# The output projection of a hybrid decoder layer, from eight dense tiles to seven block products

## The chip, the cores and the metric

The kernel runs on one core of a Trainium2 chip. A core has five engines that run their own instruction streams and meet only at semaphores: TensorE (PE, with its weight loads PEld), VectorE (DVE), ScalarE (ACT), GpSimd (POOL) and SyncE (SP, which only issues transfers here). The measure is the device time of one execution in microseconds (us), the median of several runs.

## The reference

One layer of a decoder, for 1024 positions of width 1024, all in float32:

```python
h = rmsnorm(x, mix_norm[l])
proj = h @ w_in[l]
q, k, v, su, sv, g_a, g_b = jnp.split(proj, splits, axis=-1)
y_att = sliding_window_attention(q, k, v, q_norm[l], k_norm[l], sinks[l])
y_sgu = chunked_spatial_gating(su, sv, sgu_norm[l], w_s[l], b_s[l])
merged = (jax.nn.sigmoid(g_a) * (y_att @ w_oa[l])
          + jax.nn.sigmoid(g_b) * (y_sgu @ w_ob[l]))
x = x + merged @ w_out[l]
x = x + conv_gated_mlp(rmsnorm(x, ffn_norm[l]), w_up[l], conv_w[l], conv_b[l], w_down[l])
```

The change is about `x + merged @ w_out` and about what it hands to the MLP: the rows of the new x times the gain `ffn_norm`, as right operands of the up projection. The RMS factor of that norm is one number per position, so it can be applied before or after the projection.

## The kernel before

Everything is kept transposed: channels on the 128 partitions, the 1024 positions along the free dimension, in two halves L and H of 512. Each float32 operand is used as a high and a low part: ACT rounds a copy (`copy_hi`), DVE or POOL subtracts it from the original, and each product is three matmuls, high x high, high x low, low x high (`mm3`, `prod`). A "split" below is this pair of a copy and a subtraction.

Most matrix products (gates, branches, up and down projection) are done in 2x2 blocks with seven products instead of eight: A11·B11, A12·B21, S1·T1, S2·T2, S3·T3, S4·B22, A22·T4, where the S are sums of weight blocks and the T sums of blocks of the right operand (`Blocks`, `Left`). For the two branch projections the S are formed in DRAM by accumulating transfers on POOL's queue (`wb_copy`, `wb_add`). The output projection alone is dense.

The stages around the change, in order:

- `gates()`: eight gate pairs, c = 0 to 7, whose tanh goes to DRAM.
- The branch projections: `B_UNITS`, eight units u of two jobs each (`branch`, `first` and `second`). A job splits a block of weights two jobs ahead, multiplies, and post-processes. The units u = 2, 4, 6, 7 belong to branch a; after each of them `m_add` adds the branches up to two row tiles of the merged matrix m and splits them into `mhi` and `mlo`, part of it late on POOL (`lo_late`). `un["hooks"]` puts further splits of the branches' right operands into the units.
- The output projection: eight jobs (`out_tile`, the last one `last_tile`), one per row tile d of 128 output channels in the order `D_ORDER`. Each is a dense product over all eight k, 48 matmuls. The first two tiles leave out k = 6 and 7, whose m comes last, and make them up later (`rest`). `post` adds the result to x, multiplies with gain and RMS factor of the first norm (`rstd_b`) into h, stores x, and forms the right operands of the MLP's up projection in `comb`: splits of B11, T1, B21, B22, T3 at once, T2 and T4 as raw sums that `first_pair` splits.
- `mlp()`: `first_pair` is the first pair of column tiles of the up projection, seven products of 12 matmuls, with the square sums of x in it (`ssq_cols`); 21 pairs follow, then the down projection.

`run_jobs` goes through the jobs: it issues the matmuls of job i, the load of job i + 4, the split for job i + 2, and what is left of job i, its post-processing. The program order of each engine is the order in which these functions are called (`tc.manual_schedule`): an instruction that waits holds back all that stand behind it on its engine. The split weights have two buffers ("wh" and "wl"), so the split for job i + 2 waits until TensorE has finished job i. SBUF has seven large slots that take turns under the tag "Y", PSUM four tiles of two banks each, from which `PS` takes the next in turn.

## Time and profile before

| | |
|---|---|
| median of 3 runs | 1174.04 us (1173.48 to 1174.11) |
| the profiled execution | 1174.47 us |
| its span | 1172.8 us |
| granted TensorE clock | 1.0 of full speed |
| bytes moved by DMA | 192.84 MB, mean 164 GB/s |
| largest idle time of TensorE from 330 to 600 us | 0.3 us, behind a POOL subtraction of weights |

How to read it: the busy time of an engine counts its instructions, not its waits. A matmul's duration in the records is longer than the distance to the next, since matmuls are pipelined; the time of a stretch of matmuls is read from first to first. In rows of a timeline the columns are start, duration, engine, line, operation, output and inputs, shape, count, and in brackets the idle time before it with what ended it. In rows of groups they are line, engine, operation, output and inputs, shapes, count, then busy time, mean duration in ns, and idle time before with what ended it. In rows of windows they are stretch, length, busy time and count of PE, PEld, DVE, ACT and POOL, the granted clock, the share of the DMA engines and GB/s. In rows of DMA issues the last columns are the size and the time from issue to landing.

### The profile page before, as it was taken

The page shows a single profiled execution, that of the slowest core. Times are in us where ns is not written, and L with a number is a line of the kernel's source. Part 1 is how long each engine was busy: PE and PEld are TensorE (multiplying, and loading weights), DVE is VectorE, ACT ScalarE, POOL GpSimd, SP SyncE. Part 2 cuts the span into 40 slices and gives each one's busy share as a digit, 9 for nine tenths or more (in the row PEclk, how much of TensorE's full clock was granted, in tenths as well). Part 3 has the DMA queues.
Part 4 walks back from the last instruction along what each step waited for, and adds up shares of the span by engine and source line. Part 5 has one row for each costly group of instructions (what it writes and reads, how often), then busy time and mean ns, then how long its engine had stood idle before and what let it go on. Part 6 is the DMA issues. An engine that isn't in the chain of part 4 may idle for free.

```text
span 1172.8 us, 15805 instructions
## 1 busy us (share of the span) xinstructions
PE 1164.2 (99%) x5832; PEld 987.3 (84%) x5832; DVE 848.3 (72%) x982; ACT 562.4 (48%) x868; POOL 631.1 (54%) x434
## 2 busy tenths in 40 slices
PE   9999999999999999999999999999999999999998
PEld 9899999888888878888888888888888888888887
DVE  6777746734446876778779778887888797875674
ACT  6665568643437543435544443444444455425231
POOL 1667574598883863454876767676767640000000
PEclk9999999999999999999999999999999999999999
DMA  9310155265737762554564545554555268966471
GB/s 365 108 37 21 64 184 190 84 203 174 203 103 254 238 203 96 180 153 126 144 167 131 146 133 162 137 163 111 171 135 162 81 209 304 363 218 198 161 234 64
DMA packets 82237, 192.84 MB, mean 164 GB/s; under 512 B 9328, under 2 KB 17008, under 8 KB 82032
## 3 DMA queue, kind: packets, MB, share of 16 engines
q1 hardware_dynamic: 74304, 171.78, 42.6%
q0 software_dynamic: 7456, 15.73, 8.4%
q10 hardware_dynamic: 400, 4.33, 1.1%
q8 instruction: 46, 0.75, 0.3%
q14 instruction: 31, 0.25, 0.1%
HBM read 151.17 MB, written 49.02 MB: 171 GB/s over the span
## 4 chain that ended last, share of the span: by engine, by line
PE 87%; DVE 4%; POOL 3%; ACT 2%; issue 2%; DMA 2%; SPq 0%; DVEq 0%; POOLq 0%; ACTq 0%
PE pz L1085 49%; PE pd L1880 10%; PE pdy L1880 8%; PE px L94 2%; PE px L92 2%; PE px L93 2%; PE pu L94 1%; PE pu L92 1%; PE pu L93 1%; PE pv L542 1%; PE pq L92 1%; PE pq L94 1%; PE pq L93 1%; PE sc L467 1%; PE sc L470 1%
## 5 line engine op out<-in xcount | busy, mean ns | idle before, releaser
L1085 PE MATMUL pz<-T,qh 128*128 128x512 f32 x472 | 145.6, 390 | 0.0
L1085 PE MATMUL pz<-B,ph 128*128 128x512 f32 x352 | 109.6, 392 | 0.1
L1085 PEld LDWEIGHTS pz<-T,qh 128*128 128x128 f32 x472 | 88.5, 188 | 18.6 <-ACT u L910 0.3
L1044 POOL TENSOR_TENSOR pl<-lp,ph 128x1024 fp32r<-128x1024 f32 x30 | 74.2, 2472 | 52.9 <-ACT ph L88 52.9
L1085 PE MATMUL pz<-T,ql 128*128 128x512 f32 x236 | 91.8, 389 | 0.0
L1044 POOL TENSOR_TENSOR ql<-lq,qh 128x1024 fp32r<-128x1024 f32 x30 | 76.7, 2557 | 9.1 <-ACT qh L88 9.1
L1085 PEld LDWEIGHTS pz<-B,ph 128*128 128x128 f32 x352 | 65.1, 188 | 15.8 <-ACT x L1720 2.8
L1103 DVE TENSOR_TENSOR pz<-pz,rstd_b 128x1024 f32<-128x1024 f32 x60 | 73.9, 1232 | 4.5 <-ACT rstd_b L142 2.5
L1085 PE MATMUL pz<-T,s3h 128*128 128x512 f32 x232 | 71.4, 389 | 0.0
L1085 PE MATMUL pz<-y,wjh 128*128 128x512 f32 x224 | 69.5, 391 | 0.6 <-POOL y L1258 0.3
L1085 PE MATMUL pz<-B,pl 128*128 128x512 f32 x176 | 68.5, 389 | 0.0
L1880 PE MATMUL pd<-bh,ah 128*128 128x512 f32 x176 | 68.5, 389 | 0.0
L1880 PE MATMUL pd<-bl,ah 128*128 128x512 f32 x176 | 68.5, 389 | 0.0
L1880 PE MATMUL pd<-bh,al 128*128 128x512 f32 x176 | 68.5, 389 | 0.0
L1085 PE MATMUL pz<-B,AX 128*128 128x512 f32 x264 | 63.4, 389 | 0.0
L1085 PE MATMUL pz<-T,AX 128*128 128x512 f32 x264 | 63.4, 389 | 0.0
L1044 POOL TENSOR_TENSOR s3l<-lq,s3h 128x512 fp32r<-128x512 f32 x20 | 26.0, 1298 | 61.3 <-ACT s3h L88 61.3
L1085 PEld LDWEIGHTS pz<-T,AX 128*128 128x128 f32 x264 | 49.6, 188 | 10.3
L1085 PEld LDWEIGHTS pz<-B,AX 128*128 128x128 f32 x264 | 49.6, 188 | 10.3
L88 ACT ACTIVATE AX<-lr 128x1024 fp32r<-128x1024 f32 x22 | 23.4, 1063 | 70.0 <-POOL lr L646 70.0
L1575 DVE SCALAR_TENSOR_TENSOR tg<-pz,cp,tg 128x1023 f32<-128x1023 f32 (+1 forms) x44 | 56.2, 1278 | 0.8
L1575 DVE SCALAR_TENSOR_TENSOR tv<-pz,cp,tv 128x1023 f32<-128x1023 f32 (+1 forms) x44 | 56.2, 1278 | 0.8
(352 smaller groups left out, 3524.2 us busy)
## 6 DMA issues: line engine op xcount, KB each, us to landing
lp<-wup SPq DMA_DIRECT2D x22, 512.0 KB, 3.7
lq<-wup SPq DMA_DIRECT2D x22, 512.0 KB, 4.1
ra<-wdown SPq DMA_DIRECT2D x44, 256.0 KB, 4.5
b<-T SPq DMA_DIRECT2D x44, 256.0 KB, 3.9
lq<-wup POOLq DMA_DIRECT2D x42, 256.0 KB, 5.3
B<-tv SPq DMA_DIRECT2D x33, 256.0 KB, 2.3
T<-tt SPq DMA_DIRECT2D x33, 256.0 KB, 2.1
b<-B SPq DMA_DIRECT2D x33, 256.0 KB, 3.7
```

Source lines behind the costliest of these rows:

```text
L88: return nc.scalar.activation(dst, src, AF.Copy, scale=scale)
L92: nc.tensor.matmul(out, wh, mh, start=first, stop=False, **kw)
L93: nc.tensor.matmul(out, wh, ml, start=False, stop=False, **kw)
L94: nc.tensor.matmul(out, wl, mh, start=False, stop=last, **kw)
L467: nc.tensor.matmul(o[g], qs[:, g, c], kTh[:, g, ks], start=t2 == 0, stop=False, skip_group_check=True)
L470: nc.tensor.matmul(o[g], qs[:, g, c], kTl[:, g, ks], start=False, stop=True, skip_group_check=True)
L542: nc.tensor.matmul(o, vhl[:, kb, g, :], w[:, 2 * g:2 * g + 2, :], start=i == 0 and g == 0, stop=i == len(ops) - 1, skip_group_check=True)
L1044: nc.gpsimd.tensor_tensor(l, r, h.bitcast(F), op=ALU.subtract)
L1085: nc.tensor.matmul(o, p[:, k, :], m, start=not more and k == 0 and j == 0, stop=k == nk - 1 and j == 2, skip_group_check=True)
L1103: nc.vector.tensor_tensor(z, z, rstd_b, op=ALU.mult)
L1575: nc.vector.scalar_tensor_tensor(t[:, j:], p[:, 0:1024 - j], cw[:, ci, 2 - j:3 - j], t[:, j:], op0=ALU.mult, op1=ALU.add)
L1880: nc.tensor.matmul(o[d], p[:, k - k0, m], q[:, k - k0, :], start=new and k == 0 and j == 0, stop=k == HK - 1 and j == 2, skip_group_check= ...
```

## The change

The output projection becomes seven block products as well, with its own order. Its matmuls run product by product: a step s takes one product over the four output tiles d of half the channels, as two jobs of two tiles each, 24 matmuls a job, so 14 jobs (numbers 16 to 29 of the list, called j = 0 to 13). The results gather in two sets of four PSUM quarters, X and Y:

- step 0: X = A11·B11, and ACT copies X to Y
- step 1: Y += A12·B21, which is quarter 11 of the result
- step 2: X += S2·T2; ACT copies X to Y; DVE keeps X with x21
- step 3: Y += S1·T1; DVE keeps Y with x22
- step 4: Y += S4·B22, which is quarter 12
- step 5: X = S3·T3, with what was kept quarter 22
- step 6: X += A22·T4, with what was kept quarter 21

The lower half comes out with the opposite sign, so that all four weight sums are additions; `final` turns it.

```diff
+    def wo_copy(j):
+        i, x = divmod(j, 2)
+        if x == 0:
+            d_wo.append(dr.tile([512, 1024], F, tag=f"wo{i}", name=f"wo{i}"))
+        nc.scalar.dma_start(d_wo[i][256 * x:256 * x + 256], a["wo"][i + x].rearrange("e p m -> (e p) m"))
+
+    def wo_add(j):
+        e, o = d_wo
+        x, y = slice(0, 256), slice(256, 512)
+        out, src = ((o[y], a["wo"][3].rearrange("e p m -> (e p) m")), (e[y], o[y]), (e[x], e[y]),
+                    (o[x], a["wo"][2].rearrange("e p m -> (e p) m")))[j]
+        nc.gpsimd.dma_start(out, src, accum_op=ALU.add, max_dma_last_dim=4096)
```

`wo_copy` is called in the gate pairs 1 to 4, `wo_add` at the start of the units 0 to 3. `m_add` no longer splits whole rows; it keeps m raw (`mraw`) and makes the block operands, some in it, some in hooks of the units 6 and 7, some in the first output jobs:

```diff
+        un["hooks"][6, "x"] = lambda: m_split("T1", 0)
+        un["hooks"][6, 0] = lambda: m_split("T1", 1)
+        un["hooks"][7, 0] = lambda: (m_split("B22", 0), m_split("B21", 0))
...
         for e, z in enumerate((q.zg, q.zv)):
             c = 2 * j + e
+            nc.vector.tensor_tensor(mraw[i][:, c % 4, :], ms.pop(c), z, op=ALU.add)
+        if i == 0:
+            m_split("B11", g)
+        else:
+            if u == 7:
+                for e in (0, 1):
+                    m_split("B21", g, ks=slice(2 * g + e, 2 * g + e + 1))
+        m_sum(("T1", "T2")[i], g)
```

The output jobs themselves, with the work that is put beside their matmuls:

```diff
+    O_STEPS = (("A11", "B11", "X"), ("A12", "B21", "Y"), ("S2", "T2", "X"), ("S1", "T1", "Y"), ("S4", "B22", "Y"),
+               ("S3", "T3", "X"), ("A22", "T4", "X"))
+    O_WORK = {
+        0: lambda: (m_split("T2", 0), out_load("11"), out_load("21")),
+        1: lambda: (m_split("T2", 1), m_split("B22", 1), out_load("22")),
+        2: lambda: (m_sum("T3", 0), m_sum("T3", 1), m_sum("T4", 0), m_sum("T4", 1), out_load("12")),
+        3: lambda: m_split("T4", 0, nc.gpsimd),
+        4: lambda: (m_split("T4", 1, nc.gpsimd), w0.load_p(), w0.load_s3(), w0.load_q()),
+        5: lambda: (b11(0), b11(1), m_split("T3", 0)),
+        6: lambda: (b11(2), b11(3), w0.adds()),
+        7: lambda: m_split("T3", 1),
+        8: lambda: w0.sums_r(),
+        9: lambda: w0.split_s3(),
+    }
+    def final(n, d, p, out, sign):
+        nc.vector.scalar_tensor_tensor(out, p, 0.5 * sign, ob[n][:, d, :], op0=ALU.mult, op1=ALU.add)
+    def o_post(s, d):
...
+        if s == 4:
+            g, ng = gain("12", d)
+            final("12", d, Yb, Yb, 1.0)
+            keep("12", d, Yb)
+            nc.scalar.activation(A, Yb, AF.Copy, scale=g)
+            stt(B, Yb, ng, B, ALU.add)
+            square("12", d, Yb, Yb)
+            right_split("T1", d, B, nc.vector)
+        if s == 5:
+            g, ng = gain("22", d)
+            final("22", d, X, Yb, -1.0)
+            right_split("B22", d, Yb, nc.vector, g)
+            keep("22", d, Yb)
+            stt(A, Yb, ng, A, ALU.add)
+            stt(B, Yb, ng, B, ALU.subtract)
+            square("22", d, Yb, Yb)
+        if s == 6:
+            g, ng = gain("21", d)
+            final("21", d, X, X, -1.0)
+            right_split("B21", d, X, nc.vector, g)
+            keep("21", d, X)
+            stt(X, X, g, B, ALU.add)
+            square("21", d, ob["21"][:, d, :], pools["fp"].tile([128, 512], F, tag="sqt", name=nm("sqt")))
...
+            O_WORK.get(j, lambda: None)()
+            yield
+            if s == 0:
+                if j == 0:
+                    ob["Y"] = [p[:, c] for p in (PS("pY"), PS("pY")) for c in (L, H)]
+                for d in (2 * e, 2 * e + 1):
+                    nc.scalar.copy(ob["Y"][d], ob["X"][d])
             else:
+                if s == 6:
+                    (w0.split_p, w0.split_q)[e]()
+                for d in (2 * e, 2 * e + 1):
+                    o_post(s, d)
+            if j == 11:
+                for d in range(4):
+                    right_split("T3", d, ob["A"][:, d, :], nc.vector)
+            if j == 12:
+                for d in range(4):
+                    right_split("T2", d, ob["B"][:, d, :], nc.vector)
```

Here `keep` is a copy on ACT and a store, `square` a square on ACT and, but for the first tile, a sum on DVE, `stt` one DVE operation, `right_split` a copy on ACT and a subtraction on the engine named. x is taken without the factor `rstd_b`, so `ssq_cols` no longer divides by it. `first_pair` has the order A11, S3, S1, A12, S4, S2, A22 and splits T4 straight from X; the MLP's first left operand is loaded and split within the output jobs instead of in a job of its own. The rotating tag "Y" becomes seven fixed slots Y0 to Y6, and the down projection takes its first four PSUM quarters from the other pool. In `run_jobs` every split now stands between a job's matmuls and its post-processing:

```diff
-        for i in range(len(jobs) - 1):
+        for i in range(len(jobs)):
             m = jobs[i][2](job_w.pop(i))
             next(m)
-            if i == 17:
-                job_split(18)
-                next(m)
-            if i:
+            if 0 < i < 16:
                 job_load(i + 4)
-            if i != 16:
-                job_split(i + 2)
-            if lo_late:
-                lo_late.pop(0)()
+            job_split(i + 2)
+            if i >= 16:
+                job_load(i + 4)
             for _ in m:
                 pass
```

349 lines of the change are left out of this document (166 added, 183 removed).

## The prediction

> **What bounds the kernel now.** I read the page first (busy time, chain of waits), then TensorE's timeline, the windows of the stages, the groups with shapes kept apart, and last the timelines of DVE, ACT and POOL where the change cuts in.
>
> ```profile
> span 1172.8 us, 15805 instructions
> ...
> PE 1164.2 (99%) x5832; PEld 987.3 (84%) x5832; DVE 848.3 (72%) x982; ACT 562.4 (48%) x868; POOL 631.1 (54%) x434
> ...
> PE 87%; DVE 4%; POOL 3%; ACT 2%; issue 2%; DMA 2%; SPq 0%; DVEq 0%; POOLq 0%; ACTq 0%
> ```
>
> TensorE is busy 99% of the span and carries 87% of the chain: a matmul taken away is time gained, and any wait put before a matmul is time lost, since no later slack gives it back.
>
> ```profile
> 447.48 0.39 PE L92 MATMUL px<-mh,wjh 128*128 128x512 f32 x1
> ...
> 535.09 0.61 PE L1085 MATMUL pz<-B,ph 128*128 128x512 f32 x2
> ...
> 555.99 0.61 PE L1085 MATMUL pz<-B,ph 128*128 128x512 f32 x2
> ```
> ```profile
> L94 PE MATMUL px<-mh,wjl 128*128 128x512 f32 x128 | 49.9, 390 | 0.3 <-POOL wjl L109 0.3
> L109 POOL TENSOR_TENSOR wjl<-wj,wjh 128x1024 fp32r<-128x1024 f32 x7 | 17.5, 2499 | 31.1 <-ACT wjh L88 31.1
> L88 ACT ACTIVATE B<-h 128x512 fp32r<-128x512 f32 x12 | 7.3, 629 | 26.5 <-DVE h L1483 20.8 <-DVE h L1523 5.7
> L1439 DVE TENSOR_TENSOR B<-h,B 128x512 fp32r<-128x512 f32 x9 | 6.0, 690 | 1.4 <-ACT B L88 1.4
> ```
>
> The output projection runs from 447.48 to 535.09: 87.6 us for 3x128 = 384 matmuls, 0.2275 us each (a record of 0.39 is a pipelined duration, not an interval), with 0.3 us idle. The first pair of the MLP takes 20.9 more, to 555.99. TensorE waits for nothing there because each dense tile lasts 48 matmuls, 10.9 us: its weight split and its post-processing fit beside it.
>
> **The change, part by part.** Times t count from the start of the output stage.
>
> *Removed:* 384 matmuls become 7 products x 4 tiles x 4 k x 3 = 336. The stage would last 336 x 0.2275 = 76.4: **-11.2 us**. Two small DVE operations in the row-norm go too; at nothing, TensorE doesn't wait for them. The job, the unit in which weights are split two ahead, halves to 24 matmuls, 5.46 us.
>
> *Prices:*
> ```profile
> 456.04 2.36 DVE L1393 TENSOR_TENSOR ml<-m,mh 128x1024 fp32r<-128x1024 f32 x2
> 478.54 1.15 ACT L88 ACTIVATE B<-h 128x512 fp32r<-128x512 f32 x2 [1.53 <-DVE h L1483]
> 479.60 0.62 ACT L88 ACTIVATE T<-h 128x512 fp32r<-128x512 f32 x1
> 424.67 2.57 POOL L1320 TENSOR_TENSOR wjl<-wj,wjh 128x512 fp32r<-128x512 f32 x2 [3.36 <-ACT wjh L88]
> 535.23 0.63 ACT L88 ACTIVATE B<-h 128x512 fp32r<-128x512 f32 x1 [2.67 <-DVE h L1523]
> 535.90 0.69 DVE L1439 TENSOR_TENSOR B<-h,B 128x512 fp32r<-128x512 f32 x1 [0.70 <-ACT B L88]
> ```
> DVE: 0.69 for 512 columns, 0.61 behind another, 1.17 for 1024. ACT: 0.53 behind another (479.60 - 478.54 for two), 0.63 alone, so about 1.0 for 1024. POOL: 1.29 a half, 2.4 for 1024. The last two rows are a **round trip**: DVE stands idle 0.70 while ACT makes the high part that DVE subtracts. The blocks are scheduled by hand, so every engine keeps the program's order.
>
> *(1) Weight sums in DRAM.* Four copies of 1 MB on ACT's queue in the gates: nothing, TensorE is full there and the eight earlier copies cost ACT only their issue. Four accumulating DMAs on POOL's queue in units 0 to 3:
> ```profile
> 385.55 4.05 POOL L1320 TENSOR_TENSOR wjl<-wj,wjh 128x512 fp32r<-128x512 f32 x2 [0.43 <-DMA wj<-wb]
> ...
> 393.90 2.40 POOL L1258 TENSOR_TENSOR y<-ta,y 128x1024 fp32r<-128x1024 f32 x1
> ```
> ```profile
> 396.35 0.50 PE L1085 MATMUL pz<-y,wjh 128*128 128x512 f32 x1 [0.26 <-POOL y L1258]
> ```
> ```profile
> wb<-wb POOLq DMA_DIRECT2D x1, 1024.0 KB, 14.4
> ```
> ```profile
> wb<-wb POOLq DMA_DIRECT2D x1, 1024.0 KB, 10.7
> ```
> ```profile
> L944 POOL DMA_DIRECT2D wb<-wb x6: 787/838/1093, 246.3 to 338.7; - x6
> ```
> TensorE already waits 0.26 for POOL's subtraction of 393.90, so there POOL's delay is TensorE's. The second add comes ahead of 385.55, the third ahead of 393.90, and the third reads what the second writes. Issued at 385.1, the second lands 10.7 to 14.4 later, 397.6 in the middle; then 0.84 to issue, 2.4 to subtract: 400.9 instead of 396.3. **+4.6 us** (2.8 to 6.5). Without that wait only two issues count, 1.3, the lower end. Behind the waiting instruction stand that subtraction and the weight splits of units 2 and 3. [...]
>
> *(2) The boundary.*
> ```profile
> 443.67 0.69 DVE L646 TENSOR_TENSOR x<-x,pz 128x512 f32<-128x512 f32 x1 [1.04 <-PE pz L1085]
> ...
> 447.98 0.68 DVE L1354 TENSOR_TENSOR pz<-x,pz 128x512 f32<-128x512 f32 x1
> ...
> 453.70 2.35 DVE L1387 TENSOR_TENSOR m<-m,pz 128x1024 f32<-128x1024 f32 x2
> ```
> ```profile
> 519.51 1.60 POOL L646 TENSOR_TENSOR lr<-lq,lp 128x512 f32<-128x512 f32 x1 [2.63 <-issue]
> 519.87 1.79 DVE L1439 TENSOR_TENSOR T<-h,T 128x512 fp32r<-128x512 f32 x1
> 521.19 1.61 POOL L646 TENSOR_TENSOR lr<-lp,lr 128x512 f32<-128x512 f32 x1
> 521.58 1.77 DVE L650 SCALAR_TENSOR_TENSOR T2f<-h,h 128x512 f32<-128x512 f32 x1
> ```
> DVE is nearly full in units 6 and 7. Added ahead of the addition of 447.98: T1's sum and splits in units 5 and 6 (they push the start at 443.67 back by 2.3, of which 1.04 was idle), and in unit 7 T2's sum and the splits of B22 and B21, 3.5, in place of a subtraction of 1.4. So 447.98 becomes 452.4, and the last sums of the branches end at 460.4 (t 12.9) instead of 456.05. ACT stands before them with B21's copies; behind these in its queue are T2's copy (1.0), the weight split of job 2 (1.0) and the copies X to Y, which job 2 accumulates onto: Y at t 16.1, POOL's first half of the low weights at 16.7. Job 2's third matmul was due at 11.4: **+5.4**. With nothing pushed back in units 5 and 6, it would be 3.0.
>
> After t 12.9 DVE has eight operations of 1.17 and two of 0.65 ahead of job 2's first `final`: B21, T2, B22, then `O_WORK[2]`'s four sums. That is t 23.6. But the last four rows show POOL and a DVE operation with both inputs in SBUF exclude each other and take turns (1.29 becomes 1.6, 0.69 becomes 1.8). Five POOL halves and their gaps fall between: t 31.2. Then ACT's six copies (to 35.2), T4's copy (36.1), POOL's T4 subtraction, which stands ahead of the weights (38.6), and a weight half, 39.9: job 5's third matmul, due at 33.2. **+6.8**, and 1.2 more for T4's other half before job 6. Without turns this part costs nothing; I take the rows. Part (2): **+13.4** (3 to 14).
>
> *(3) Post-processing and first pair.* Count from the end of job 8, step 4's first half (t' = 0). Per tile d, in order on DVE:
> - step 4: `final`, `stt`, wait for ACT's three operations, square sum, T1's low part: 3.7. Four tiles and a weight split between: to 15.3.
> - step 5: `final` 0.7, round trip 0.7, low part, two `stt` (0.61 each), round trip for the square 0.7, sum 0.65: 4.6. To 33.7; T3's four low parts to 36.2.
> - step 6: `final`, round trip, low part, `stt`, sum: 3.3.
>
> A job gives two tiles 5.46; these need 7.4, 9.2 and 6.6. TensorE waits because step 6 accumulates onto X, which step 5's `final` must have read: the last tile's at t' 29.8, so the stage ends at 32.6 instead of 27.3. Next late is the MLP's first left operand: `split_p` stands on ACT behind T3's copies (36.35), POOL adds 2.4: t' 38.85, product to 41.1. S3·T3 to 43.85. `split_q` stands on ACT behind step 6's first half (to 42.8) and T2's copies, so to 45.3; POOL waits for T2's last low part and adds 2.4: 47.8, S1·T1 to 50.1, A12·B21 to 52.8. `split_r` stands behind step 6's second half (ACT's last square at 51.1), x1's copy and two of T4's (52.7), takes 1.0 on ACT and 2.4 on POOL: S4·B22's third matmul at 56.15. Then 10 matmuls, S2·T2, the 1.8 of the square sums and A22·T4: 65.6, against 27.3 + 20.9 = 48.2. **+17.4 us.** Ends: with DVE's 63 operations (15 in step 4, 20 in step 5, 16 in step 6, 12 low parts) at 0.65 and no round trip it has 41 us of work where 43.7 are left before A22·T4: 0 to 3. Above: `split_r` also waits for a row's store out of its slot, +2. I take 17.4, since the round trip is a row.
>
> *(4) At nothing:*
> ```profile
> 447.50:535.00 87.50, 87.23 (x385) 71.94 (x384) 62.82 (x57) 28.32 (x37) 36.94 (x21) 1.00 0.45 142
> ```
> 3 MB more weight loads, under a DMA share of 0.45 in this stage (next to last column); fixed slots; the psum rotation of the last stage. If that cover fails, a late weight load costs what it is late.
>
> Sum: -11.2 + 4.6 + 13.4 + 17.4 = **+24.2**. The profiled execution took 1174.47 (span 1172.8 and 1.67 around); that is 0.43 above the median of 1174.04, so 1198.2.
>
> **Rivals.**
> 1. *The posts keep pace* (faster). If a tile's post goes at DVE's issue interval, 0.61, because ACT's copies are ready when DVE comes to them, steps 4 to 6 need at most 5 x 0.61 = 3.1 a tile, and DVE's backlog stays off the weights: -11.2 + 1.3 + up to 4, 1164 to 1168. It decides at 2.73 us per tile. For it: DVE is only 72% busy overall, and the posts of before cause no wait of TensorE. Against: the 0.70 idle in the row of 535.90.
> 2. *Half the loss.* The queues catch up in the MLP's first pair or the turns are not taken: 0 to 5 of part (2), 8 to 12 of part (3): 1175 to 1186.
> 3. *It cancels.* One part alone bites, about 11 us: 1172 to 1176.
> 4. *DMA congestion adds.*
> ```profile
> 381.00:390.00 9.00, 9.00 (x41) 7.46 (x40) 8.08 (x9) 6.02 (x9) 8.57 (x6) 1.00 0.73 234
> ```
> ```profile
> q0 software_dynamic: 7456, 15.73, 8.4%
> ```
> The DMA's share is 0.7 there already. The page gives the software queue 15.73 MB and 8.4% of the span, 6.3 us of all engines per MB; four adds are 25 us of all engines where 0.3 of the some 40 us of units 0 to 3 is free, 12. Late weights could add 6: up to 1208. It is the top of my range.
>
> That the products aren't saved is no rival: the loops count 336.
>
> **How the numbers follow.** Forecast, with congestion inside, 1186 to 1208: 0.62. Half the loss: 0.14. Cancels: 0.08, nearly all of it within 0.2%. Posts keep pace: 0.16. A measurement tells 0.2%, 2.3 us, from no change. Faster 0.16, same 0.07, slower 0.77. Range 1172 to 1208, which leaves out the faster case and a little above.
>
> **What would show it.** Right: TensorE idle about 4 us before S2·T2 of unit 2, released by POOL; 5 before the second step, released by ACT or POOL; a gap in job 5 behind T4; gaps of 2 in step 6 released by DVE; and 3 to 7 before A11, S1 and S4 of the first pair, released by POOL. Wrong: 336 matmuls in under 80 us, or a first pair of 21. What would break it most is an order on DVE or ACT other than the program's.

## The result, and the profile after

The change makes the kernel slower: 1227.16 us, median of 6 runs (1223.01 to 1230.37), beside 1174.07 (1173.48 to 1176.15) for the kernel before. The ratio is 1.045, with a 95% interval from 1.0429 to 1.0472. Forecast were 1198.2 with a range up to 1208: the sign was right, the size, +53.1 instead of +24.2, was not, and the time lies outside the range.

The profiled execution of the kernel after took 1226.57. Its page, with the span, TensorE's busy time, the granted clock in 40 slices and the chain by engine:

```profile
span 1224.7 us, 15874 instructions
...
PE 1171.8 (96%) x5784; PEld 988.5 (81%) x5784; DVE 861.1 (70%) x1019; ACT 594.8 (49%) x938; POOL 642.5 (52%) x448
...
PEclk9999999999999999987999999999999999999999
...
PE 75%; DVE 9%; ACT 5%; POOL 5%; issue 3%; DMA 2%; DVEq 0%; ACTq 0%; POOLq 0%
```

The 48 matmuls are gone (5832 became 5784), so the expected 11.2 us were saved. But TensorE's share of the chain fell from 87% to 75%, and DVE's rose from 4% to 9%. The second surprise is in the clock line: two slices, between 520 and 582 us, stand below 9.

TensorE's timeline of after, all waits over 1.4 us between 370 and 600 us (start, duration, ..., and in brackets the wait before the row and what ended it):

```profile
401.57 0.50 PE L1099 MATMUL pz<-y,wjh 128*128 128x512 f32 x1 [2.60 <-POOL y L1275]
...
419.22 0.73 PE L1099 MATMUL pz<-y,wjh 128*128 128x512 f32 x2 [2.58 <-ACT x L1356]
...
442.69 0.73 PE L1099 MATMUL pz<-y,wjh 128*128 128x512 f32 x2 [2.51 <-ACT x L1356]
...
475.19 1.22 PE L1611 MATMUL pY<-mB,wjh 128*128 128x512 f32 x2 [3.25 <-ACT pY L1620]
...
494.79 0.73 PE L1611 MATMUL pX<-mT,wjh 128*128 128x512 f32 x2 [1.56 <-ACT wjh L88]
...
497.93 0.50 PE L1611 MATMUL pX<-mT,wjl 128*128 128x512 f32 x1 [2.41 <-POOL wjl L1542]
...
546.36 1.19 PE L1611 MATMUL pX<-mT,wjh 128*128 128x512 f32 x2 [7.75 <-DVE pY L1509]
...
557.51 1.19 PE L1611 MATMUL pX<-mT,wjh 128*128 128x512 f32 x2 [3.78 <-DVE pY L1509]
...
583.49 1.22 PE L1099 MATMUL pz<-T,s3h 128*128 128x512 f32 x2 [13.64 <-ACT x L1735]
```

These nine sum to 40.1. With six more (1.35 us at 277.87 in the gates, and five of 0.4 to 0.9) the waits of TensorE from 250 to 640 us come to 44.9; in the kernel before they were 0.7.

The rows that follow the last of these waits, from the same timeline:

```profile
584.51 0.63 PE L1099 MATMUL pz<-T,s3l 128*128 128x512 f32 x1
584.93 1.05 PE L1099 MATMUL pz<-T,s3h 128*128 128x512 f32 x2
...
587.49 0.63 PE L1099 MATMUL pz<-T,s3h 128*128 128x512 f32 x2
587.96 0.39 PE L1099 MATMUL pz<-T,s3l 128*128 128x512 f32 x1
```

From 584.51 to 584.93 one matmul takes 0.42 us; from 587.49 to 587.96 two take 0.47. So behind the wait TensorE first runs at half speed. Read row by row, seven such stretches follow the waits, lasting 3.4 to 6.1 us and losing 1.5 to 2.9 us each against 0.2275 us a matmul, together 12.9 us. Behind the waits of 2.58, 2.51 and 2.41 the stretch begins only 0.8 to 1.5 us after the wait. The windows of the output stage with the first pair, before and then after, show the same in the clock (next to the DMA share):

```profile
460.00:565.00 105.00, 104.73 (x478) 86.96 (x477) 76.43 (x72) 41.53 (x56) 52.76 (x31) 1.00 0.47 141
```
```profile
460.70:565.90 105.20, 85.92 (x337) 68.00 (x337) 72.14 (x83) 57.18 (x97) 50.92 (x34) 0.90 0.43 143
565.90:605.50 39.60, 23.76 (x101) 18.42 (x101) 17.16 (x27) 16.54 (x27) 12.29 (x8) 0.83 0.33 93
```

The account of the span's +51.9 is then: -11.2 matmuls, +44.2 waits (44.9 - 0.7), +12.9 half speed, and 6.0 not followed further. No engine became a bound: DVE is busy 72 of 105 us in the stage that stalls. It waits as well.

### The profile page after: what moved, and what is told of

It reads as the page before. It is cut to its first block, busy times and chain, and to the rows that moved or that the text cites. A ratio compares the mean times of both kernels' runs of the same rounds, so it can differ in the third digit from the quotient of the medians.

```text
span 1224.7 us, 15874 instructions
## 1 busy us (share of the span) xinstructions
PE 1171.8 (96%) x5784; PEld 988.5 (81%) x5784; DVE 861.1 (70%) x1019; ACT 594.8 (49%) x938; POOL 642.5 (52%) x448
## 4 chain that ended last, share of the span: by engine, by line
PE 75%; DVE 9%; ACT 5%; POOL 5%; issue 3%; DMA 2%; DVEq 0%; ACTq 0%; POOLq 0%
PE pz L1099 44%; PE pdx L1962 10%; PE pd L1962 7%; DMA lq<-wga 1%; PE pu L94 1%; PE pu L92 1%; PE pu L93 1%; PE pv L542 1%; POOL pl L1058 1%; PE pq L92 1%; PE pq L94 1%; PE pq L93 1%; PE pY L1611 1%; POOL lr L646 1%; DVE mraw L1438 1%
## 5 line engine op out<-in xcount | busy, mean ns | idle before, releaser
L1962 PE MATMUL pdx<-bh,ah 128*128 128x512 f32 x176 | 68.6, 390 | 0.1
L1962 PE MATMUL pdx<-bh,al 128*128 128x512 f32 x176 | 68.5, 389 | 0.0
L1962 PE MATMUL pdx<-bl,ah 128*128 128x512 f32 x176 | 68.5, 389 | 0.0
L1099 PEld LDWEIGHTS pz<-T,s3h 128*128 128x128 f32 x232 | 44.4, 192 | 23.4 <-ACT x L1735 14.1
L1340 POOL TENSOR_TENSOR wjl<-wj,wjh 128x512 fp32r<-128x512 f32 (+1 forms) x32 | 39.1, 1243 | 41.7 <-ACT wjh L88 41.7
L646 DVE TENSOR_TENSOR pz<-pz,u 128x512 f32<-128x512 f32 x37 | 25.9, 700 | 45.7 <-ACT u L1111 39.4
L1058 POOL TENSOR_TENSOR AX<-lr,AX 128x1024 fp32r<-128x1024 f32 x22 | 53.5, 2432 | 8.6 <-ACT AX L88 8.6
```

Of the source, the lines that this page charges most:

```text
L646: eng.tensor_tensor(out, x, y, op=op)
L1058: nc.gpsimd.tensor_tensor(l, r, h.bitcast(F), op=ALU.subtract)
L1099: nc.tensor.matmul(o, p[:, k, :], m, start=not more and k == 0 and j == 0, stop=k == nk - 1 and j == 2, skip_group_check=True)
L1340: nc.gpsimd.tensor_tensor(l[:, k], r[:, k], h[:, k].bitcast(F), op=ALU.subtract)
L1962: nc.tensor.matmul(o[d], p[:, k - k0, m], q[:, k - k0, :], start=new and k == 0 and j == 0, stop=k == HK - 1 and j == 2, skip_group_check= ...
```

## The experiments

Line numbers are those of each kernel's own code, so they shift a little. The times of experiments 1 to 8, 11 and 14 are of one run each, and after's own six runs spread by 7.4 us; a single time within that spread of another says little, so there the waits of TensorE are read. In brackets behind a time: the kernel before on the same chip.

### Does a wait cost more than its length? (e1_holes)

The kernel before, with copies of a PSUM tile onto itself put on ACT ahead of the second use of that tile in four units: 4, 7, 10 and 16 of them, to make waits of different lengths where nothing else changes.

```diff
+            for _ in range({1: 4, 3: 7, 5: 10, 6: 16}.get(u, 0)):
+                nc.scalar.copy(q.g0, q.g0)
             q.prod(q.v0, "S3", "T3")
```

> The kernel before, with 4, 7, 10 and 16 copies of a result in place on ScalarE ahead of the second use of the same accumulator in units 1, 3, 5 and 6: four holes in TensorE's row of products, and nothing else changed. A copy of a 128x512 tile in PSUM takes 0.58 us in the trace after, so the holes should be about 1.5, 3, 5 and 8.5 us, some 18 us together. Theory (a hole of 2.5 us or more is followed by 3.4 to 3.8 us of matmuls at half clock): the matmuls after the last three holes come every 0.43 us in place of 0.227 for about 3.5 us, 1.7 us is lost behind each, and the span grows by the sum of the holes and a further 5 to 7 us; behind the hole of 1.5 us nothing is lost. Rival (the clock of the kernel after fell for another reason): the matmuls after each hole come every 0.227 us at once, and the span grows by the sum of the holes alone.

1200.88 (1175.98), so +24.9, while the four waits sum to 19.94. TensorE's timeline at the first and the fourth wait:

```profile
384.66 0.74 PE L1085 MATMUL pz<-y,wjh 128*128 128x512 f32 x2 [1.64 <-ACT pz L1336]
385.24 0.39 PE L1085 MATMUL pz<-y,wjl 128*128 128x512 f32 x1
385.47 0.62 PE L1085 MATMUL pz<-y,wjh 128*128 128x512 f32 x2
...
455.75 1.22 PE L1085 MATMUL pz<-y,wjh 128*128 128x512 f32 x2 [9.55 <-ACT pz L1336]
456.77 0.63 PE L1085 MATMUL pz<-y,wjl 128*128 128x512 f32 x1
457.19 1.05 PE L1085 MATMUL pz<-y,wjh 128*128 128x512 f32 x2
```

Behind 1.64 a matmul takes 0.23 us at once (385.24 to 385.47); behind 9.55 it takes 0.42 (456.77 to 457.19). Behind the waits of 3.47, 5.28 and 9.55 the stretches at half speed lose 1.7, 2.0 and 1.6 us, behind that of 1.64 there is none: the loss hangs on there being a hole, hardly on its length. 19.94 and these 5.2 (before rounding) make 25.1, beside the 24.9 measured. This loss stands in no term of the prediction.

### Part 1: the weight sums (e3_no_sums)

After without the transfers of the weight sums; the output leaves out the sums (single blocks stand in their place).

```diff
-        if c < 5:
-            wo_copy(c - 1)
...
-            if u < 4:
-                wo_add(u)
...
-            src = d_wo[o][256 * x + 128 * e:256 * x + 128 * e + 128]
+            src = a["wo"][2 * o + x, e]
```

> The kernel after without the eight copies and sums of output weights in DRAM: the output stage loads blocks as they are, so the output leaves out the weight sums. Theory (the waits in units 3 to 6 come from VectorE's added work, those at the gates and in unit 2 from the copies and sums): the waits of 2.58 and 2.51 us ahead of the second use of the first accumulator stay, those of 1.35 and 2.60 go, the share of the DMA engines from 372 to 421 us falls from about 1.0 to about 0.7, and the kernel takes 1217 to 1223 us. Rival (the transfers also slow the loads that the units and the boundary wait for): all four go, the boundary's waits shrink too, and it takes under 1212 us.

1220.21 (1175.98). The wait in the gates is gone and that of 2.60 in unit 2 is 0.3; those of 2.58 and 2.51 in units 3 and 5 stand unchanged, and so does the 3.25 at the boundary. So the first two belong to the sums' transfers, the second as forecast, and the two in units 3 and 5 do not. The share of the DMA engines from 372 to 421 us fell to 0.64 without the transfers (1.03 in after), and the boundary's waits did not shrink (3.25, 2.98 and 1.92 beside 3.25, 1.56 and 2.41), so the crowded DMAs had not made them. POOL's timeline of after shows the mechanism:

```profile
388.03 0.86 POOL L957 DMA_DIRECT2D wo<-wo  x1
...
398.17 0.88 POOL L957 DMA_DIRECT2D wo<-wo  x1 [1.29 <-DMA wo<-wo]
398.77 2.75 POOL L1275 TENSOR_TENSOR y<-ta,y 128x1024 fp32r<-128x1024 f32 x1
```

The third add waits until the second has landed, 10.1 us after that one's issue, and the subtraction that TensorE waits for at 401.57 stands behind it.

### Units 3 and 5 (e5_units)

Here are DVE and then ACT of after, ahead of the wait of 2.58 that ended at 419.22:

```profile
414.10 1.22 DVE L1416 TENSOR_TENSOR mB<-mraw,mB 128x1024 fp32r<-128x1024 f32 x1 [1.20 <-ACT mB L88]
415.36 1.22 DVE L646 TENSOR_TENSOR mraw<-mraw 128x1024 f32<-128x1024 f32 x1
416.50 0.69 DVE L1376 TENSOR_TENSOR pz<-x,pz 128x512 f32<-128x512 f32 x1
```
```profile
417.28 0.59 ACT L1377 COPY u<-pz 128x512 f32<-128x512 f32 x1 [3.28 <-DVE pz L1376]
417.76 0.94 ACT L88 ACTIVATE wjh<-wj 128x512 fp32r<-128x512 f32 x2
418.60 0.58 ACT L1356 COPY x<-pz 128x512 f32<-128x512 f32 x1
```

`m_add` splits B11 and sums T1 in these units. The two DVE operations, and 1.20 us in which DVE waits for ACT's high part, stand ahead of the addition at 416.50; ACT's copy of that tile waits for the addition, and the copy that frees TensorE's tile stands behind it. The experiment moves the low part of B11 and T1's sum to other units and the weight sums into the attention stage.

```diff
         if i == 0:
-            m_split("B11", g)
+            m_hi("B11", g)
...
-        m_sum(("T1", "T2")[i], g)
+        if i:
+            m_sum("T2", g)
...
+        un["hooks"][3, 1] = lambda: m_lo("B11", 0)
+        un["hooks"][4, 0] = lambda: m_sum("T1", 0)
```

> The kernel after with the eight transfers of the weight sums moved to the attention stage (the DMA engines stand idle from 30 to 150 us), and VectorE's low part of B11 and its T1 sum moved from units 3 and 5 to units 4 and 6, where VectorE has some 2 us to spare; the low part of the second half of T1 goes to GpSimd. Theory (the four waits of 1.35, 2.60, 2.58 and 2.51 us up to the end of the units are queue order: transfers in the way of a load and of GpSimd, added work in the way of VectorE's first sum): each falls under 0.7 us, three holes and their half clock go, and the kernel takes 1210 to 1216 us. Rival (VectorE's load as a whole is too large for the units wherever the work stands): waits of over 2 us come back in units 4 to 7 and the kernel takes 1218 us or more, what the run without sums took.

1218.79 (1174.63). All four waits ahead of unit 6 are under 0.3; one of 3.09 came at 438.42, behind a DVE addition. That is the outcome the rival named: the mechanism stands for units 3 and 5, but the work that was moved stalled another unit, and the 8.4 us returned are less than expected.

### The boundary (e7_boundary)

The same for the first output jobs: `O_WORK` in another order, the splits of B22 behind jobs 2 and 3, those of T2 behind the copies X to Y.

```diff
-        0: lambda: (m_split("T2", 0), out_load("11"), out_load("21")),
-        1: lambda: (m_split("T2", 1), m_split("B22", 1), out_load("22")),
+        0: lambda: (out_load("11"), out_load("21")),
+        1: lambda: (m_sum("T2", 0), m_sum("T2", 1), out_load("22")),
+        2: lambda: (m_split("B22", 0), out_load("12")),
+        3: lambda: m_split("B22", 1),
```

> The kernel after with the work between the units and the output stage in another order: the copies of the first quarters ahead of the splits on ScalarE, the sums of T2 to T4 and the splits of B22 spread over jobs 1 to 7, half of B21 and T4 on GpSimd, and job 2 taking the rows of B21 that come first. Theory (the waits of 3.25, 1.56 and 2.41 us at jobs 2 and 5 are ScalarE's and GpSimd's queues behind VectorE's sums): they fall to under 2 us together and the kernel takes 1217 to 1222 us. Rival (the work of the boundary is too much in any order): the same microseconds are waited at jobs 5 to 10, and it stays within 3 us of 1227.

1228.46 (1174.63), no gain by the time, as the rival had it. The waits of 3.25, 1.56 and 2.41 are gone, and one of 4.00 came at 504.21, for the copies X to Y of step 2, with 4.28 us in which ACT waited for DVE's `final` ahead of it. More than half of the delay went on to the next instruction in DVE's queue. Waits in the gates and in unit 2, which the edit doesn't touch, were 3.7 us longer in this run (3.73, 2.24 and 1.72 beside 1.35 and 2.60), so the time alone says little.

### Part 3: the post-processing (e2_x1_early, e4_sbuf, e6_tail)

DVE and ACT of after during step 5, one tile from `final` to `final`:

```profile
545.51 0.70 DVE L1509 SCALAR_TENSOR_TENSOR pY<-pX,ac 128x512 f32<-128x512 f32 x1
546.97 0.75 DVE L1496 SCALAR_TENSOR_TENSOR B<-pY,cp,B 128x512 fp32r<-128x512 f32 x1 [0.76 <-ACT B L88]
548.37 0.75 DVE L1521 SCALAR_TENSOR_TENSOR hA<-pY,ng,hA 128x512 f32<-128x512 f32 x1 [0.66 <-ACT ac L1505]
549.04 0.74 DVE L1521 SCALAR_TENSOR_TENSOR hB<-pY,ng,hB 128x512 f32<-128x512 f32 x1
550.43 0.69 DVE L1518 TENSOR_TENSOR sq<-sq,pY 128x512 f32<-128x512 f32 x1 [0.65 <-ACT pY L1517]
551.03 0.69 DVE L1509 SCALAR_TENSOR_TENSOR pY<-pX,ac 128x512 f32<-128x512 f32 x1
```
```profile
546.24 0.69 ACT L88 ACTIVATE B<-pY,cp 128x512 fp32r<-128x512 f32 x1 [1.49 <-DVE pY L1509]
547.75 0.59 ACT L1505 COPY ac<-pY 128x512 f32<-128x512 f32 x1 [0.82 <-DVE B L1496]
```

The tile takes 5.5 us: five DVE operations and three waits for ACT, not two. The additional one is ACT's copy `ac` for the store. It and DVE's operations only read pY, yet ACT begins when DVE has ended (0.82) and DVE when ACT has (0.66): on a PSUM quarter the two engines go in turn even as readers. TensorE's wait at 546.36 ended with the `final` of 545.51, that at 557.51 with the last tile's.

e4_sbuf lets `final` write into SBUF, so that all further reads come from there, and drops the copy for the store:

```diff
-        nc.scalar.copy(ob[n][:, d, :], p)
...
-            final("22", d, X, Yb, -1.0)
-            right_split("B22", d, Yb, nc.vector, g)
+            R_ = ob["22"][:, d, :]
+            final("22", d, X, R_, -1.0)
+            right_split("B22", d, R_, nc.vector, g)
```

> The kernel after with the last part of the change undone: each final quarter is written to its tile in SBUF, from which it is stored, split, summed and squared, in place of standing in PSUM; the copy for the store goes. Theory (VectorE and ScalarE take turns at one PSUM tile, so their times add up: 5.6 us for a tile of step 5 of which VectorE's own work is 3.6): step 5 takes 3.6 to 4.2 us a tile, step 6 3.0 to 3.6, the waits of 7.75 and 3.78 us at products 12 and 13 fall to under 5 together, that of 13.64 to 6 to 10, and the kernel takes 1207 to 1217 us. Rival (VectorE's own work or the order of the posts binds): step 5 stays above 5 us a tile and the kernel within 3 us of 1227.

1216.82 (1175.98): the waits of 7.75, 3.78 and 13.64 became 3.17, 1.84 and 9.90. DVE's timeline of e4_sbuf, in which only the first of the three waits is left; the two `final` are 4.1 us apart:

```profile
547.00 0.68 DVE L1508 SCALAR_TENSOR_TENSOR ac<-pX,ac 128x512 f32<-128x512 f32 x1
548.47 0.75 DVE L1496 SCALAR_TENSOR_TENSOR B<-ac,cp,B 128x512 fp32r<-128x512 f32 x1 [0.79 <-ACT B L88]
...
551.06 0.68 DVE L1508 SCALAR_TENSOR_TENSOR ac<-pX,ac 128x512 f32<-128x512 f32 x1
```

Two of the four tiles of step 5 still took 4.9 and 5.1 us: in each of them one DVE operation with two inputs in SBUF lasted 1.55 or 1.77 instead of 0.75 while POOL worked beside it.

e2_x1_early asks about the 13.64: S3·T3 waited for ACT's copy `x1`, which reads the other half of its PSUM tile and stood behind the posts of the last job. Here the product A11·B11 and that copy come ahead of those posts.

```diff
                 if s == 6:
                     (w0.split_p, w0.split_q)[e]()
+                if j == 13:
+                    psum["P"] = [psA, psA, psC_[0], psC_[0]]
+                    fp_head()
```

> The kernel after, with the first pair's first product and the copy of its result (x1) put ahead of the last two tiles' post-processing on ScalarE. Theory (the wait of 13.64 us is the place of that copy in ScalarE's queue): it falls to 2 to 5 us, some 3 to 6 us come back at the fourth product, which needs the splits of step 6, and the kernel takes 1217 to 1222 us. Rival (the work of step 6 on VectorE and ScalarE binds the first pair wherever the copy stands): the same time is waited at the fourth product, and the kernel stays within 2 us of 1227.

1229.25 (1175.98), no gain by the time. The 13.64 became 4.47, and 4.51 came at 592.89, for a copy of another product behind the same posts. 4.7 us of waiting were saved, but two holes stand where one stood. Waits in the gates and in unit 2, which the edit doesn't touch, were 3.1 us longer in this run (3.38 and 3.69 beside 1.35 and 2.60).

e6_tail does all of it: quarters in SBUF, posts phase by phase for two tiles at a time (all `final` first, then the copies, then the sums), and the first pair's products reordered.

```diff
-                for d in (2 * e, 2 * e + 1):
-                    o_post(s, d)
+                o_posts(s, (2 * e, 2 * e + 1))
...
+        for d in ds:
+            final(n, d, X[d] if s in (2, 5, 6) else Yb[d], Q[d], 1.0 if s in (1, 4) else -1.0)
```

> The kernel after with the quarters in SBUF, as in the run of that name, and the posts of two tiles taken phase by phase (both final sums first, VectorE's sums ahead of what waits for ScalarE), the first pair's first three products with their copies ahead of the last posts, the product with B21 moved behind those with B22 and T2, and the split weights of S2 and S4 put into two load buffers. Theory (the tail's waits of 7.75, 3.78 and 13.64 us are turns at PSUM and places in two queues; VectorE's own work for step 5 is 3.6 us a tile and for all three steps less than what TensorE has to do up to the last product): they fall to under 8 us together, and the kernel takes 1203 to 1209 us. Rival (the sum of VectorE's and ScalarE's work binds): it does no better than the quarters in SBUF alone, 1214 to 1218 us, with the wait at the products with B21 and T4.

1209.60 (1174.63), just above the range expected. The tail's waits are 2.43, 2.06, 1.72, 5.45 and 1.21, and 2.37 at 615.97: 15.2 where after's seven waits from 546 to 633 us sum to 28.2.

### All together (e8_all, e9_all2, e10_all3)

e8_all has the edits of e5_units, e6_tail and e7_boundary.

> The three edits of the runs beside it together. Theory (the stalls are separate, each with its price and its 1.7 us of half clock): the savings add, about 14, 20 and 7 us, and the kernel takes 1180 to 1192 us. Rival (they share a cause, such as VectorE's total work): the sum is worth less than the largest alone and some 5 us, over 1198 us.

1204.21 (1174.63), more than the theory allowed and where the rival had it. One wait of 10.33 came at 506.61. DVE and POOL of e8_all ahead of it:

```profile
493.83 10.30 DVE L1500 TENSOR_TENSOR B<-hB,B 128x512 fp32r<-128x512 f32 x2
```
```profile
492.76 3.21 POOL L1549 TENSOR_TENSOR wjl<-ow,wjh 128x512 fp32r<-128x512 f32 x2
495.28 2.98 POOL L1421 TENSOR_TENSOR mT<-mraw,mT 128x1024 fp32r<-128x1024 f32 x1
497.60 3.09 POOL L1549 TENSOR_TENSOR wjl<-ow,wjh 128x512 fp32r<-128x512 f32 x2
```

Two DVE operations with both inputs in SBUF, 1.3 us of work, lasted 10.30 while POOL ran without a pause, up to 503.58. Moving the results to SBUF had taken DVE from the turns with ACT into turns with GpSimd.

e9_all2 and e10_all3 move queues again, first T1's, T3's and T4's sums and the first pair's splits, then step 6's posts into the first pair:

```diff
-        2: lambda: (m_split("B22", 0), out_load("12")),
-        3: lambda: m_split("B22", 1),
+        2: lambda: (m_sum("T4", 0), m_sum("T4", 1), out_load("12")),
+        3: lambda: (m_sum("T3", 0), m_sum("T3", 1)),
```
```diff
+                    o_posts(6, (0, 1))
+                if j != 12:
+                    o_posts(s, (2 * e, 2 * e + 1))
```

> All three edits, with what their traces showed mended: GpSimd's splits of T4 and T1 go to VectorE (in the run of all three edits two VectorE operations of 0.63 us each took 10.30 us while GpSimd worked without a gap, and the wait of 10.33 us at job 8 came of it), T1's second sum and splits stand behind the unit's own sums, the final sums of the last tiles stand ahead of the squares, squares of neighbouring tiles go to different memories, and the splits of the first pair's weights stand earlier in ScalarE's queue. Theory (what is left over the kernel before is queue order, 1.7 us of clock a hole, and turns of VectorE and GpSimd at SBUF): of the 29.5 us of waits less than 9 stay, in at most three holes, and the kernel takes 1168 to 1178 us, near the kernel before and up to 0.5% below it. Rival (VectorE's work for the last three steps, about 46 us with the first pair's sums against 48 us of TensorE's time, does not fit): the waits come back in the first pair, over 12 us in all, and it takes 1180 to 1195 us.

> The run before it had 1189.0 us with four holes that count, 2.38, 2.96, 7.44 and 2.09 us, and 1163 us is the kernel before less the 48 products: 18.75 us of waits and four times 1.7 us of clock make up the 26 us between. Here the copy x1 stands ahead of step 6's splits on ScalarE, the final sums of the last two tiles of step 5 ahead of the other sums of the first two on VectorE, the splits of B22 behind the copies of job 4, and the squares of step 1 go to SBUF. Theory (each hole is a place in a queue): the holes of 7.44, 2.96 and 2.38 us go, or fall under 1.5 us each, and the kernel takes 1168 to 1176 us, between 0.5% below and 0.2% above the kernel before. Rival (VectorE is full from step 4 on, so what is pulled forward pushes something else back): holes of over 6 us in all come back in the first pair's last products, and it takes 1177 to 1186 us.

1189.03, ratio 1.0118 (1.0097 to 1.0139), and 1190.02, ratio 1.0133 (1.0116 to 1.0150): the first where the rival had it, the second above even the rival's range. Waits over 0.6 of 16.7 and 17.1 us remained, but in other places: 2.38, 2.96 and 7.44 at 482, 526 and 546 in the one, 3.69, 3.28 and 6.27 at 496, 534 and 551 in the other. An order that clears one place fills another, which spoke for a cause that follows DVE.

### The turns with GpSimd (e11_no_low, e14_after_no_low, e12_mix, e13_dve_low)

e11_no_low is e10_all3 without GpSimd's low parts of the weights in the output stage and the first pair; the high part stands for the low one, so that it counts twice. e14_after_no_low leaves out the same in after.

```diff
             copy_hi(h[:, k], r[:, k])
-            nc.gpsimd.tensor_tensor(l[:, k], r[:, k], h[:, k].bitcast(F), op=ALU.subtract)
-        return h, l
+        return h, h
```

> The run before it (1190.0 us) with GpSimd's low parts of the weights left out in the output stage and in the first pair: the third product of each block takes the high part again, so the output is coarser, and TensorE's, VectorE's and ScalarE's instructions are all still there. Theory (VectorE's operations with both operands in SBUF stand still while GpSimd works: from 460 to 565 us they took some 23 us more than their usual time, such as 6.90 us for four T3 splits of 0.63 each): these times return to 0.6 to 0.75 us for a tile, the holes of 3.69, 3.28 and 6.27 us fall to under 5 us together, and the kernel takes 1172 to 1180 us. Rival (VectorE's own work is what does not fit): the times return, but over 9 us of holes stay, and it takes 1183 us or more.

> The kernel after with GpSimd's low parts of the weights left out in the output stage and in the first pair; the third product of each block takes the high part a second time, so the output is not the reference's. Theory (in the kernel after, with its quarters in PSUM, the turns with GpSimd cost the boundary, and the turns with ScalarE the tail): the waits for low parts at jobs 5 and 8 and at the first pair, 2.41, 0.40 and 0.73 us, go, those of 7.75, 3.78 and 13.64 us stay within 2 us each, and the kernel takes 1216 to 1223 us. Rival (GpSimd's turns set the tail's pace there too): these three fall to under 12 us together and it takes less than 1212 us.

e11_no_low took 1170.28 (1174.63), 20 us less than e10_all3, with waits of 2.08 and 2.40 and none else over 0.7. DVE's rows for the same four low parts of T3, in e10_all3 and then in e11_no_low:

```profile
536.62 6.90 DVE L1500 TENSOR_TENSOR T<-hA,T 128x512 fp32r<-128x512 f32 x4
```
```profile
523.14 2.49 DVE L1503 TENSOR_TENSOR T<-hA,T 128x512 fp32r<-128x512 f32 x4
```

and POOL in e10_all3 meanwhile:

```profile
537.08 2.47 POOL L1063 TENSOR_TENSOR q<-lq,q 128x1024 fp32r<-128x1024 f32 x1 [7.88 <-ACT q L88]
539.51 2.85 POOL L1063 TENSOR_TENSOR r<-lr,r 128x1024 fp32r<-128x1024 f32 x1
```

e14_after_no_low took 1222.23, 0.8 below the fastest of after's runs. The waits for low parts are gone, but those for `final` are 8.69 and 3.03, and S3 waits 15.62. So in after itself GpSimd's low parts are worth about 5 us by the times (1227.16 - 1222.23), less than the spread of 7.4 us; its tail is the turns with ACT. The turns with GpSimd decide once those with ACT are removed.

e12_mix goes halfway: it takes step 6 from PSUM again, where DVE's operations kept 0.67 to 0.75 us beside GpSimd in after. It also moves a copy, squares and splits at the three holes of e10_all3.

```diff
-        Q = {d: ob[n][:, d, :] for d in ds}
+        Q = {d: X[d] if s == 6 else ob[n][:, d, :] for d in ds}
```

> The run of 1190.0 us with its three holes dealt with one by one: the copy u2 ahead of the splits of step 6, the squares of step 5 away from the PSUM tiles that the first pair takes, the splits of B11 and of half of T3 and T4 behind the final sums they stood ahead of; and the quarter of step 6 used from PSUM again, as the change has it, so that VectorE's operations on it have one operand there and need not wait for GpSimd. Theory (places in queues and the turns with GpSimd): of 19.4 us of waits under 9 stay, and the kernel takes 1172 to 1180 us. Rival (VectorE is full from step 4 on): the holes move behind the first pair's last products, over 11 us in all, and it takes 1183 to 1190 us again.

1192.21, ratio 1.0152 (1.0139 to 1.0166), a little above the rival's range. The turns with ACT returned: around the low parts of step 6 DVE waited 0.76 for ACT and ACT 0.82 for DVE each time, and a wait of TensorE of 8.34 for a copy on ACT came at 556.57.

e13_dve_low gives the low parts to DVE itself, from the third split of the output weights on and in the first pair, in 1.2 us per 1024 columns instead of GpSimd's 2.4, and moves some copies, splits and squares to where DVE now comes to them.

```diff
-            nc.gpsimd.tensor_tensor(l, r, h.bitcast(F), op=ALU.subtract)
+            (nc.vector if self.i == 0 else nc.gpsimd).tensor_tensor(l, r, h.bitcast(F), op=ALU.subtract)
...
+        if n_split[0] > 2:
+            lows.append(lambda: nc.vector.tensor_tensor(l, r, h.bitcast(F), op=ALU.subtract))
```

> The run of 1190.0 us with the low parts of the weights of the output stage and of the first pair formed on VectorE in place of GpSimd (some 20 us of work more for the engine that is full, 27 us less for the one that is not), the copies u2 and x7 ahead of the last splits on ScalarE, the splits of the first pair's second weights and of B11 moved to where they hold nothing up, and the squares of step 5 away from PSUM. Theory (an operation on GpSimd costs VectorE more, by standing still, than the same operation costs it when it does it itself): VectorE's operations have their usual times, under 12 us of waits stay, and the kernel takes 1174 to 1184 us. Rival (20 us more do not fit on VectorE): the holes grow, and it takes 1192 us or more.

1177.04, median of 11 runs, ratio 1.0018 (1.0009 to 1.0027). 13 us came back, from giving *more* work to the engine whose lateness made the waits. Windows of e10_all3 and of e13_dve_low (the fifth and the seventh column are the busy times of DVE and POOL):

```profile
460.00:565.00 105.00, 90.26 (x377) 72.25 (x376) 93.35 (x98) 58.19 (x95) 53.08 (x33) 0.93 0.43 132
```
```profile
460.00:565.00 105.00, 96.95 (x426) 79.75 (x425) 89.76 (x120) 63.13 (x101) 17.38 (x13) 0.95 0.46 146
```

In the same 105 us DVE did 22 more instructions in less busy time. What fell is the length of DVE's operations with two inputs in SBUF: in this window the low parts of T3 went from a mean of 1.78 us to 0.69, those of B11 from 1.59 to 0.69, the sums into hA from 1.55 to 0.75, while `final`, with one input in PSUM, stayed at 0.68. How much of the 13 us came from the moves in e13_dve_low is not told apart. One long wait was left, of 6.22 at 548.71, for a low part of T4.

### The last wait (e15_last, e16_end)

e15_last puts the last square sums on GpSimd, T4's high parts first, and the square sums' matmuls behind A22·T4; e16_end takes the sums back to DVE, behind T4's low parts.

```diff
-            nc.vector.tensor_tensor(q, q, p, op=ALU.add)
+            (nc.gpsimd if n == "21" else nc.vector).tensor_tensor(q, q, p, op=ALU.add)
...
-        ratio = ssq_cols(pb)
...
         q.prod(q.v0, "A22", "T4", more=True)
+        ratio = ssq_cols(pb)
```

> The run of 1177.0 us (waits of 1.62 us at the first pair's first product and 6.22 us at its sums of squares) with the low part of that pair's first weights ahead of other sums on VectorE, all high parts of T4 ahead of its low parts (ScalarE and VectorE took turns at the PSUM tiles, 0.66 us each), the last four squares summed on GpSimd, which has nothing else there, while VectorE splits T4 from PSUM, and the sums of squares behind the last product. Theory (VectorE, relieved of GpSimd's turns, is late by its own chain alone, so 3 us off the chain are 3 us off the time): 1.5 us and 3 to 4 us go, and the kernel takes 1170 to 1174 us, faster than the kernel before by 0.1 to 0.4%. Rival (the wait only passes to the next product, or GpSimd's four sums hold VectorE up again): 1175 to 1180 us.

> The run before it (1180.6 us) with its new waits undone: the four last squares are summed on VectorE again, behind the low parts of T4 (GpSimd's four sums had held VectorE's four sums of T4 up, 5.90 us in place of 3.0), GpSimd's power for the norm stands ahead of the next pair's low parts again (a wait of 5.13 us), and the high parts of T2 stand ahead of the copies u2 and x7 on ScalarE (1.42 us). Theory (VectorE's chain and nothing else is left): one wait of 3 to 5 us stays at the first pair's last product, and the kernel takes 1171 to 1175 us. Rival (the end of the output stage is full on VectorE, and 1177 us is what the order can give): 1176 to 1179 us.

1180.59, ratio 1.0043 (1.0030 to 1.0056), and 1180.00, ratio 1.0043 (1.0029 to 1.0056): both worse than e13_dve_low and above what was expected. POOL and DVE of e15_last:

```profile
540.64 6.41 POOL L1525 TENSOR_TENSOR sq<-sq,ac 128x512 f32<-128x512 f32 x4 [54.65 <-ACT ac L1524]
```
```profile
542.49 5.90 DVE L1528 SCALAR_TENSOR_TENSOR pX<-ac,cp,hB 128x512 f32<-128x512 f32 x4
```

The same four DVE operations took 3.01 in e13_dve_low. Waits of 1.42, 3.44, 1.63 and 5.13 took the place of the 6.22. In e16_end DVE's four sums took 5.38 instead of 3.07, with GpSimd's low part of the next pair beside them, and TensorE waited 4.92 for them. No version that does the whole work beat the kernel before; e13_dve_low came nearest, 0.2% behind it.

## Why the prediction was wrong in its size

**The removed matmuls.** -11.2 was right: 48 fewer, and where nothing waits they still take 0.23 us each.

**(1) The weight sums, +4.6: right mechanism, smaller.** The wait stood where it was forecast, behind the add that needs the one before, and was 2.60: the add landed 10.1 us after its issue, where the middle of 12.6 was taken. That one add waits for the landing of another, on which the 4.6 rests, no run of before shows; after's POOL row does, with 1.29 us idle behind the transfer. The copies in the gates, costed at nothing, made a wait of 1.35. e3_no_sums removed both.

**(2) The boundary, +13.4: right places, too large.** TensorE waited 3.25 ahead of the second step (5.4 forecast), 1.56 + 2.41 in job 5 (6.8), and nothing in job 6 (1.2): 7.2, and 0.40 at 533. The turns with GpSimd were there: in after's DVE timeline the seven operations from 475.00 up to the first `final` at 488.43 took 3.44, 2.31, 3.44 and 4.55 us, 13.7 where 1.17 each would make 8.2, so 5.5 of the 7.6 us that the prediction added. What it had too late is where they start: DVE's last sums of the branches ended at 471.4, 10.7 us into the stage, instead of 12.9.

**Not in the sum: units 3 and 5.** The prediction took the work added to units 5, 6 and 7 only as a delay of the boundary, and passed over unit 3, where `m_add` puts B11's split and T1's sum for the first time. In units 3 and 5 that work cost 2.58 + 2.51, shown by the rows of DVE and ACT above and by e5_units.

**(3) Post-processing and first pair, +17.4: right mechanism, too small; here the forecast failed.** The tile's cycle was too short in all three steps: 4.55 instead of 3.7 in step 4, 5.5 instead of 4.6 in step 5, 4.1 instead of 3.3 in step 6. What failed is the step "final, round trip, low part, two stt, round trip": it has a round trip only where one engine needs the other's result, and the copy for the store, which only reads, was costed at nothing. It is a round trip too. Four tiles each of 0.85, 0.9 and 0.8 make 10.2 us. The prediction's own marks say the same. The first `final` of step 4, on DVE, and the last square of step 6, on ACT, in after:

```profile
521.62 0.70 DVE L1509 SCALAR_TENSOR_TENSOR pY<-pY,ac 128x512 f32<-128x512 f32 x1 [4.15 <-PE pY L1611]
```
```profile
582.33 0.63 ACT L1517 ACTIVATE sqt<-ac 128x512 f32<-128x512 f32 x1
```

From the one's start (t' = 0) to the other's end are 61.3 us where 51.1 were forecast, 10.2 more. e4_sbuf took the reads out of PSUM and dropped that copy; the cycle of step 5 fell to between 4.1 and 5.1, and three waits shrank by 10.3 together.

The path was wrong too. The first pair ended at 605.71, t' 84.1 instead of 65.6, so the part cost 35.9 us instead of 17.4. The forecast had A11, S1 and S4 waiting 3 to 7 for POOL; A11 waited 0.73, and the long wait, 13.64, was S3's for ACT. The prediction let S3·T3 run from 41.1, right behind A11, though by its own marks the copy `x1` stands behind ACT's last square at 51.1. With S3·T3 and what follows behind that copy its marks would give some 69.9, an estimate from its own terms, 4.3 of the 8.3 us that the longer cycles leave; half speed behind the 13.64 makes 2.0, and the rest was not followed. e2_x1_early shows that moving this copy doesn't cure it: the next copy stands behind the same posts.

**The term that was missing: half speed behind a hole.** 12.9 us in all. The prediction counted the length of waits, not their number. e1_holes shows it in the kernel before, without any part of the change. Not all of it adds to the time: from 522 to 588 us no row of DVE or ACT waits for TensorE, so the two stretches behind the 7.75 and the 3.78, 4.7 us, only shortened the wait that came next. The other 8.3 add.

Term by term against the waits: (1) 4.0 instead of 4.6, (2) 7.6 with the 0.40 instead of 13.4, units 3 and 5 5.1 instead of 0, (3) 28.2 instead of 17.4: 44.9 beside 35.4, or 44.2 without the 0.7 that the kernel before waits. By luck (2) and units 3 and 5 nearly cancel. Of the 27.7 us between forecast and measured span, 8.8 are waits, 12.9 half speed, and 6.0 not followed. Congestion of the DMAs, the top of the range, shows in a DMA share of 1.03 from 372.7 to 421.0 (0.69 before), but no wait there ended with a load, and e3_no_sums took the congestion away without shrinking the boundary's waits.

The rival that the posts keep pace fell with the 5.5 us a tile, twice the 2.73 from which it decides. e11_no_low, one run without the whole work, took 1170.28: the seven products may gain where GpSimd's low parts cost nothing. With all work in, the gain of 11.2 was met by waits of 8.5 and half speed of 3.6 in the best version.

## What to carry to other kernels

When TensorE is 99% busy, count the holes that a change makes, not only their sum: here every one of 3.47 us or more, and most of 2 us or more, was followed by a stretch at half speed that lost about 1.4 us or more. Where the chain of another engine sets the time, that loss only shortens the next wait (4.7 us of it in after). Before work is put beside a full engine, look at what stands behind each new instruction in its queue, and count a hand-over between DVE and ACT for every pair of accesses to one PSUM tile, reads too (0.65 to 0.82 us each here). An idle engine isn't free help: low parts that GpSimd made in its own time cost more than the same low parts on the busy DVE (1190.02 us beside 1177.04, the moves of e13_dve_low included).

## What the runs showed of the hardware

**The clock.** Behind waits of 2.51 to 13.64 us in after, and behind 1.56 and 2.41 close together, matmuls came every 0.42 us for 3.4 to 6.1 us, at a granted clock of 0.50, then every 0.23. The wait of 2.60 was followed by no such stretch, those of 2.58 and 2.51 were: it isn't the length alone. The traces of all the runs, from 240 to 645 us, say it more sharply. Every wait of 3.47 us or more was followed by such a stretch, begun at once or within 1.3 us. The longest without one was 3.41 (e14_after_no_low, at 477.00), the shortest that stood alone in front of matmuls of 512 columns and had one was 1.70 (e2_x1_early, at 571.39). And the same wait of 2.58 in unit 3 had one in after, e7_boundary and e14_after_no_low, but none in e2_x1_early, e3_no_sums, e4_sbuf and e6_tail. Why equal waits differ, no run here shows.

**DVE beside GpSimd.** Four DVE operations with both inputs in SBUF took 2.49 alone and 6.90 with two GpSimd operations beside them, two took 10.30 beside a GpSimd that didn't pause. The operations `final`, with one input in PSUM, kept 1.27 to 1.29 for two. In after, from 240 to 640 us, 73 DVE operations of 128x512 with an input in PSUM had GpSimd beside them for over 80% of their time: they took 0.67 to 0.75 us, where those without it took 0.68 to 0.76.

**DVE beside ACT on one PSUM tile.** Two readers of one quarter went in turn, at 0.65 to 0.82 us for each hand-over. Whether the chip or the program's own ordering asks for it, no run here tells apart.
